# A decoder layer on one Trainium2 core: the second gate of the merge applied in the branch projection, sigmoids written as one plus tanh, and named buffers in place of a ring

## The chip, the cores and the metric

The kernel runs on one core of a Trainium2 chip. Its time is the device time of one launch in microseconds (us); for the kernel before, the median of three runs is 1783.04 us (1782.25 to 1786.08). The engines are named as the profile names them: PE multiplies matrices (PEld is its weight load), DVE and ACT work on vectors, POOL is the third vector engine and also issues some DMAs, and SP issues the other DMAs. A bank is one PSUM tile of 128x512 fp32, in which matmuls accumulate.

## The reference

One layer on 1024 positions of width 1024. What matters here is the gated merge of two attention branches:

```
proj = rms_norm(h) @ w_in                 # also gate_a, gate_b (1024 each)
o_a  = multi-head latent attention        # 1024 x 512
o_b  = stick-breaking attention           # 1024 x 512
merged = sigmoid(gate_a) * (o_a @ w_br_mla) + sigmoid(gate_b) * (o_b @ w_br_sb)
h = h + merged @ w_out
h = h + swiglu(rms_norm(h));  h = h + sigmoid(h @ w_ple_gate) * rms_norm(p @ w_ple_proj)
out = rms_norm(h)
```

## The kernel before

**Layout and precision.** Activations lie transposed: 128 features on the partitions, positions along the row, in two halves of 512. Every fp32 product is made of three matmuls on split operands: `split` (L130-132) writes a high part with a cast on ACT (L131) and the rest with a subtraction on DVE (L132), and `passes` (L134-139) multiplies high by high (L137), high by low (L138) and low by high (L139). One product over four blocks of 128 is thus 12 matmuls of 128x512.

**The order.** The code is written stage by stage; a scheduler sorts the instructions of each engine by a cost model and by priorities, and each engine then runs its list in order. A tile is a buffer from a pool; a tile whose tag has `bufs=n` shares n buffers in rotation, and a load into it waits until the earlier user is done. DMAs issued by SP and by POOL stand in the lists of these engines in the same way.

**The stages around the change.** In the input projection the two gates go to DRAM as `d_gate` (rows 0 to 1023 are gate_a, 1024 to 2047 gate_b); the stick-breaking attention leaves its heads in `d_oT`. Then comes the latent attention (MLA), head by head: `mla_proj` (L572) with weights loaded by SP (L537 w_q_b, L539 w_kv_b, one buffer for both), `mla_weights` (L601: scores, exponentials on ACT, a scaling on POOL at L637), `mla_values` (L642: transposes, casts, products). While it runs, `br_sb_unit` (L678-691) fills PE's gaps at a very low priority: for each of 8 blocks `dc` of 128 output features it loads a block of w_br_sb, splits it, and for each half makes 12 matmuls into a `pb` bank (the bank M, of which there is one), copies the bank to `bo` with ACT (L690), and stores `bo` to `d_br` by a DMA on POOL's queue (L691). The projected branch B, not yet gated, so waits in DRAM for the merge.

**The merge** works with the pool `bg`: eight slots of 16 KB per partition, one ring tag (L744-746), so that the n-th tile takes the slot that the (n-8)-th leaves. For each of four blocks `dc` of the first half of the features, `gates_in` (L753) loads a block of w_br_mla and fills one slot `gt` with gate_a, branch B and gate_b (L759, L760, L761; 512 KB each). `wo_units` (L764) loads blocks k of w_out into `woraw` (L769, two buffers) and splits them into slots `wo`. `merge` (L772) splits its weights, takes two sigmoids of 128x1024 on ACT (L778), multiplies the second with branch B on POOL (L779), and for each half makes a `pb` product of 12 matmuls, multiplies it by the first gate (DVE, L785), adds the gated branch (DVE, L786) and splits the sum into `mT`. When four blocks are merged, the products `po` of `mT` with `wo` (12 matmuls per bank, 16 banks) are made, added to the input (L808) and stored; this is the first half of the sum over k. The second half loads and merges blocks 4 to 7 while those run (L810-814), and its products come in `out_group` (L894, the addition at L903), among the start of the feed-forward stage. `pb` and `po` rotate through five banks.

The same ring later holds weights and activations (`wpj`, `spare`, `b1` to `b7`, `hs`, `wpg`).

Of the kernel before, what the change touches and what calls it, by code (L numbers as in the profile page):

```python
# [51 lines left out]
def decoder_layer(ctx: ExitStack, tc: tile.TileContext, x, p, positions, g_mix, w_in, g_q_a, w_q_b,  # L52
# [104 lines left out]
    with ExitStack() as att:  # L157
# [340 lines left out]

        with ExitStack() as ml:
            lastp = pool(late, "lastpair", side="right")  # L500
            oah = lastp.tile([P, S], F32R, name="oah")
            oal = lastp.tile([P, S], F32R, name="oal")

            def slot(tag, name, dtype=F32R):
                return qkp.tile([P, S], dtype, name=name, tag=tag, bufs=2 if tag == "vst" else 3)
# [172 lines left out]
            def br_sb_unit(dc):  # L678
                raw = bp.tile([P, 4, P], F32, name="braw", tag="braw", bufs=2)
                with tc.issue_after(fence[0]):  # L680
                    nc.sync.dma_start(out=raw, in_=w_br_sb[:, dc * P:(dc + 1) * P].rearrange("(k p) n -> p k n", p=P))
                wh = bp.tile([P, 4, P], F32R, name="bwh", tag="bwh", bufs=2)
                wl = bp.tile([P, 4, P], F32R, name="bwl", tag="bwl", bufs=2)
                split(wh, wl, raw)
                for hf in range(2):
                    s = slice(hf * HALF, (hf + 1) * HALF)
                    pb = ps.tile([P, HALF], F32, name="pb", **M)
                    passes(pb, [((wh[:, k, :], wl[:, k, :]), (obh[:, k, s], obl[:, k, s])) for k in range(4)])
                    go = bp.tile([P, HALF], F32, name="bo", tag="bo", bufs=2)
                    nc.scalar.copy(out=go, in_=pb)  # L690
                    nc.gpsimd.dma_start(out=d_br[dc * P:(dc + 1) * P, s], in_=go)  # L691

# [71 lines left out]
    def wo_units(kh):  # L764
        for k in range(4 * kh, 4 * kh + 4):
            if k % 2 == 0:
                wo[k // 2] = slot("wo", [P, 2, 2, D])
            raw = wk.tile([P, D], F32, name="woraw", tag="woraw", bufs=2)
            nc.sync.dma_start(out=raw, in_=w_out[k * P:(k + 1) * P, :])  # L769
            split(wo[k // 2][:, 0, k % 2, :], wo[k // 2][:, 1, k % 2, :], raw)  # L770

    def merge(dc, raw, g):  # L772
        kh = dc // 4
        wh = oap.tile([P, 4, P], F32R, name="wh", tag="wh", bufs=2)
        wl = oap.tile([P, 4, P], F32R, name="wl", tag="wl", bufs=2)
        split(wh, wl, raw)
        for i in range(2):
            nc.scalar.activation(out=g[:, i, :], in_=g[:, i, :], func=AF.Sigmoid)  # L778
        nc.gpsimd.tensor_tensor(out=g[:, 2, :], in0=g[:, 2, :], in1=g[:, 1, :], op=ALU.mult)  # L779
        for hf in range(2):  # L780
# [3 lines left out]
            u = g[:, 0, s]  # L784
            nc.vector.tensor_tensor(out=u, in0=pb, in1=u, op=ALU.mult)  # L785
            nc.vector.tensor_tensor(out=u, in0=u, in1=g[:, 2, s], op=ALU.add)  # L786
            split(mT[hf, kh][:, 0, dc % 4, :], mT[hf, kh][:, 1, dc % 4, :], u)
# [5 lines left out]

    gs = [gates_in(i) for i in range(4)]
    for hf in range(2):
        mT[hf, 0] = slot(f"mT{hf}0", [P, 2, 4, HALF])
    wo_units(0)
    for i in range(4):
        merge(i, *gs[i])

    gs1 = [gates_in(4 + i) for i in range(4)]
    for hf in range(2):
        for f in range(NK):
# [3 lines left out]
            out_products(po, 0, hf, f)  # L807
            nc.vector.tensor_tensor(out=st, in0=po, in1=st, op=ALU.add)  # L808
            nc.sync.dma_start(out=d_h[f * P:(f + 1) * P, hcol(hf)], in_=st)
    for hf in range(2):  # L810
        mT[hf, 1] = slot(f"mT{hf}1", [P, 2, 4, HALF])
    wo_units(1)
# [340 lines left out]
    for i in (1, 2, 6, 5, 7, 3, 4):  # L1153
# [125 lines left out]
```

## Time and profile before

| | |
|---|---|
| median of three runs | 1783.04 us (1782.25 to 1786.08) |
| the profiled execution | 1785.67 us, its span 1784.0 us |
| mean granted clock of PE | 0.981 |
| DMA traffic | 222.16 MB, mean 125 GB/s |
| MLA stage, with the filler `br_sb_unit` | about 560 to 819 us |
| first half of the merge, up to its last `pb` product | about 821 to 836 us |

The page of the profile gives busy times per engine over the whole span. A row of a timeline is: start, duration, engine, line, operation, output and inputs, count, and in brackets how long the engine had stood idle before it and what ended that. A row of a tile gives min/median/max of the durations in ns. A row of the windows gives the window, its length, then for each engine busy time and count of instructions, then the granted clock of PE (1.00 is full), the share of the DMA engines that was busy and GB/s. Matmuls overlap: the duration of one is longer than the distance from its start to the next.

### The profile page before, as it was taken

What the parts mean: (1) busy time and instruction counts of PE and PEld (TensorE: products, weight loads), DVE (VectorE), ACT (ScalarE), POOL (GpSimd) and SP (SyncE); (2) the same over time, 40 slices, a digit from 0 to 9 for tenths busy, and PEclk for the clock granted to TensorE, in tenths of its full rate; (3) what the DMA queues carried; (4) which work ended last, traced back from release to release, by engine and by line L of the source; (5) the groups of instructions that cost most, each with busy time, mean ns of one, the idle gap of its engine ahead of it and who ended that gap; (6) DMA issues with size and microseconds to landing.
All of it is one profiled execution on the core that took longest, in us unless ns stands there. A gap on an engine that the chain in (4) does not pass through costs nothing.

```text
span 1784.0 us, 23325 instructions
## 1 busy us (share of the span) xinstructions
PE 1697.2 (95%) x8148; PEld 1410.5 (79%) x8148; DVE 1157.2 (65%) x2063; ACT 901.7 (51%) x1748; POOL 389.7 (22%) x401
## 2 busy tenths in 40 slices
PE   6999999999998999996999899899999999999996
PEld 5888878888786888885889777688888878887795
DVE  6667788778885766686468765754444545557656
ACT  5266676767774777775335633233333334445411
POOL 2011320000210533342202623334434310000000
PEclk9999999999999999998999899999999999999998
DMA  5212221213314210215953475853223328565522
GB/s 171 55 58 48 59 60 42 82 45 90 115 42 138 72 61 31 83 58 200 346 205 115 143 257 180 277 168 100 95 89 118 113 101 300 191 198 164 165 67 79
DMA packets 168249, 222.16 MB, mean 125 GB/s; under 512 B 23170, under 2 KB 99970, under 8 KB 168130
## 3 DMA queue, kind: packets, MB, share of 16 engines
q1 hardware_dynamic: 162098, 200.73, 34.6%
q0 software_dynamic: 6032, 19.93, 3.1%
q8 instruction: 64, 1.05, 0.2%
q14 instruction: 55, 0.45, 0.1%
HBM read 151.93 MB, written 67.90 MB: 123 GB/s over the span
## 4 chain that ended last, share of the span: by engine, by line
PE 74%; DVE 9%; issue 6%; DMA 5%; POOL 2%; ACT 2%; SPq 1%; POOLq 0%; DVEq 0%; ACTq 0%
PE pt L137 5%; PE pt L138 5%; PE pt L139 5%; PE pd L138 4%; PE pd L137 4%; PE pd L139 4%; PE pP L139 3%; PE pP L137 3%; PE pP L138 3%; DMA spare<-w_ffn_down 2%; PE po L137 2%; PE tp L651 2%; PE po L138 2%; PE po L139 2%; PE pg L139 2%
## 5 line engine op out<-in xcount | busy, mean ns | idle before, releaser
L137 PE MATMUL pt<-nTh,w_h 128*128 128x512 f32 (+1 forms) x480 | 192.5, 402 | 3.4 <-ACT go L355 2.4
L138 PE MATMUL pt<-nTl,w_h 128*128 128x512 f32 (+1 forms) x480 | 190.1, 396 | 0.0
L139 PE MATMUL pt<-nTh,w_l 128*128 128x512 f32 (+1 forms) x480 | 189.0, 395 | 0.0
L132 DVE TENSOR_TENSOR wl<-raw,wl 128x512 fp32r<-128x512 f32 x132 | 95.4, 723 | 101.9 <-ACT wl L131 101.4
L139 PE MATMUL pP<-b,wl 128*128 128x512 f32 x352 | 139.8, 399 | 10.1 <-DVE wl L132 10.1
L131 ACT CAST wl<-raw 128x512 fp32r<-128x512 f32 x132 | 82.0, 622 | 129.2 <-PE pP L139 59.0
L137 PE MATMUL pP<-b,wl 128*128 128x512 f32 x352 | 140.2, 398 | 5.0 <-DVE t L968 3.2
L138 PE MATMUL pP<-b,wl 128*128 128x512 f32 x352 | 139.3, 396 | 0.0
L137 PEld LDWEIGHTS pt<-nTh,w_h 128*128 128x128 f32 (+1 forms) x480 | 90.7, 189 | 26.1 <-ACT go L355 5.8
L139 PEld LDWEIGHTS pt<-nTh,w_l 128*128 128x128 f32 (+1 forms) x480 | 90.6, 189 | 19.7
L138 PEld LDWEIGHTS pt<-nTl,w_h 128*128 128x128 f32 (+1 forms) x480 | 90.9, 189 | 18.5
L138 PE MATMUL pd<-drs,dls 128*128 128x512 f32 x296 | 102.0, 390 | 1.0 <-DVE drs L132 1.0
L139 PE MATMUL pd<-drs,dls 128*128 128x512 f32 x296 | 101.7, 389 | 0.0
L132 DVE TENSOR_TENSOR drs<-drr,drs 128x512 fp32r<-128x512 f32 x74 | 50.8, 690 | 78.1 <-ACT drs L131 78.1
L137 PE MATMUL pd<-drs,dls 128*128 128x512 f32 x296 | 100.7, 392 | 0.4 <-ACT dls L131 0.4
L131 ACT CAST drs<-drr 128x512 fp32r<-128x512 f32 x74 | 45.9, 623 | 105.0 <-PE pd L139 98.3
L637 POOL TENSOR_SCALAR pw<-pw,st 128x128 f32<-128x128 f32 (+5 forms) x48 | 75.0, 1569 | 71.6 <-DVE st L633 20.2
L139 PEld LDWEIGHTS pP<-b,wl 128*128 128x128 f32 x352 | 67.4, 192 | 28.2 <-DVE wl L132 13.9
L137 PEld LDWEIGHTS pP<-b,wl 128*128 128x128 f32 x352 | 67.7, 192 | 20.1 <-DVE t L968 4.1
L138 PEld LDWEIGHTS pP<-b,wl 128*128 128x128 f32 x352 | 67.6, 192 | 14.3
L445 DVE TENSOR_TENSOR sz<-sz,T 128x512 f32<-128x512 f32 (+2 forms) x96 | 52.2, 550 | 34.6 <-PE T L443 33.8
L356 POOL DMA_DIRECT2D d_gate<-go x32 | 17.8, 556 | 260.3 <-ACT go L355 221.2
(371 smaller groups left out, 4821.9 us busy)
## 6 DMA issues: line engine op xcount, KB each, us to landing
d_g<-t SPq DMA_DIRECT2D x74, 256.0 KB, 2.0
drr<-d_g SPq DMA_DIRECT2D x74, 256.0 KB, 2.8
w_raw<-w_in SPq DMA_DIRECT2D x33, 512.0 KB, 4.2
raw<-w_ffn_gate SPq DMA_DIRECT2D x11, 1024.0 KB, 5.6
raw<-w_ffn_up SPq DMA_DIRECT2D x11, 1024.0 KB, 5.5
spare<-w_ffn_down SPq DMA_DIRECT2D x44, 256.0 KB, 3.7
d_w<-spare SPq DMA_DIRECT2D x44, 256.0 KB, 3.6
drr<-d_w SPq DMA_DIRECT2D x44, 256.0 KB, 2.6
```

The lines of the kernel that those rows point to most:

```text
L131: nc.scalar.copy(out=h, in_=src)
L132: eng.tensor_tensor(out=l, in0=src, in1=r32(h), op=ALU.subtract)
L137: nc.tensor.matmul(ps, lhsT=ah, rhs=bh, start=first and i == 0, stop=False, **kw)
L138: nc.tensor.matmul(ps, lhsT=ah, rhs=bl, start=False, stop=False, **kw)
L139: nc.tensor.matmul(ps, lhsT=al, rhs=bh, start=False, stop=last and i == n - 1, **kw)
L356: nc.gpsimd.dma_start(out=dst, in_=go[0:rows, :])
L445: nc.vector.tensor_tensor(out=sz[:, c0:], in0=sz[:, c0:], in1=T[:, c0:], op=ALU.subtract)
L637: nc.gpsimd.tensor_scalar(out=pw[:, 0:nk], in0=pw[:, 0:nk], scalar1=st[:, 6:7], scalar2=None, op0=ALU.mult)
L651: nc.tensor.transpose(tp[:, i * P:(i + 1) * P], rows[i][:, kb * P:(kb + 1) * P], ident)
```

## The change

Line numbers of the changed kernel stand in square brackets.

1. **The second gate moves into `br_sb_unit`.** The unit loads its half of gate_b (256 KB, into `bo`, now three buffers, SP's queue, [L691]), ACT takes tanh(0.5 x) of it in place ([L692]), and DVE evacuates the bank with (tanh + 1) * pb in one instruction ([L697]), where ACT copied it before. POOL stores the result as before ([L698]). `d_br` now holds twice the gated branch.
2. **Sigmoids as one plus tanh.** sigmoid(x) is (1 + tanh(x/2)) / 2. In `merge` one tanh of 128x1024 on ACT ([L790]) replaces two sigmoids, the POOL product is gone, and DVE's (tanh + 1) * pb ([L796]) replaces the multiplication. The merged rows are twice too large; the factor 0.5 is put into the two additions behind the products `po` ([L819] and [L914], a scalar_tensor_tensor where a tensor_tensor was).
3. **Loads of the merge.** A `gt` slot now holds gate_a and gated branch B of two blocks, so four blocks take two slots, and gate_b isn't loaded there.
4. **The activation table** that holds exp and tanh is loaded at the start of the MLA stage ([L500]). The program has six table loads before and after; the one that stood ahead of the sigmoids (L778) is the one that is now at [L500].
5. **Named slots.** Each tile of `bg` names one of eight tags with one buffer each, so that it waits for one given predecessor: `gt` 0 and 1, `mT` of the first half 2 and 3, `wo` 4 and 5 (in both halves), `mT` of the second half 6 and 7; later `wpj` 3, `spare` 2, `b1, b2, b5, b6, b7, b3, b4` in 0, 1, 6, 7, 4, 5, 3, `hs` in 2, 3, 6, 7, `wpg` in 0, 1, 4, 5.

```diff
+            tc.keep_in_program_order(nc.scalar.preload_act_table_set("exp_and_others"))
...
                 split(wh, wl, raw)
+
+                go = []
+                for hf in range(2):
+                    go.append(bp.tile([P, HALF], F32, name="bo", tag="bo", bufs=3))
+                    with tc.issue_after(fence[0]):
+                        nc.sync.dma_start(out=go[hf], in_=d_gate[D + dc * P:D + (dc + 1) * P, hcol(hf)])
+                    nc.scalar.activation(out=go[hf], in_=go[hf], func=AF.Tanh, scale=0.5)
                 for hf in range(2):
                     s = slice(hf * HALF, (hf + 1) * HALF)
                     pb = ps.tile([P, HALF], F32, name="pb", **M)
                     passes(pb, [((wh[:, k, :], wl[:, k, :]), (obh[:, k, s], obl[:, k, s])) for k in range(4)])
-                    go = bp.tile([P, HALF], F32, name="bo", tag="bo", bufs=2)
-                    nc.scalar.copy(out=go, in_=pb)
-                    nc.gpsimd.dma_start(out=d_br[dc * P:(dc + 1) * P, s], in_=go)
+                    nc.vector.scalar_tensor_tensor(out=go[hf], in0=go[hf], scalar=1.0, in1=pb, op0=ALU.add, op1=ALU.mult)
+                    nc.gpsimd.dma_start(out=d_br[dc * P:(dc + 1) * P, s], in_=go[hf])
...
-    def slot(name, shape, dtype=F32R):
+    def slot(i, name, shape, dtype=F32R):
 
-        return bg.tile(shape, dtype, name=name, tag="big", bufs=8)
+        return bg.tile(shape, dtype, name=name, tag=f"big{i}", bufs=1)
...
-        t = slot("gt", [P, 4, S], F32)
-        ds = slice(dc * P, (dc + 1) * P)
-        nc.sync.dma_start(out=t[:, 0, :], in_=d_gate[ds, :])
-        nc.sync.dma_start(out=t[:, 2, :], in_=d_br[ds, :])
-        nc.sync.dma_start(out=t[:, 1, :], in_=d_gate[D + dc * P:D + (dc + 1) * P, :])
-        return raw, t
+        t = slot(i, "gt", [P, 2, 2, S], F32)
+        raws = []
+        for j in range(2):
+            ds = slice((dc + j) * P, (dc + j + 1) * P)
+            raws.append(w_in_branch(dc + j))
+            nc.sync.dma_start(out=t[:, j, 0, :], in_=d_gate[ds, :])
+            nc.sync.dma_start(out=t[:, j, 1, :], in_=d_br[ds, :])
+        return [(raws[j], t[:, j]) for j in range(2)]
...
-        for i in range(2):
-            nc.scalar.activation(out=g[:, i, :], in_=g[:, i, :], func=AF.Sigmoid)
-        nc.gpsimd.tensor_tensor(out=g[:, 2, :], in0=g[:, 2, :], in1=g[:, 1, :], op=ALU.mult)
+        nc.scalar.activation(out=g[:, 0, :], in_=g[:, 0, :], func=AF.Tanh, scale=0.5)
...
-            nc.vector.tensor_tensor(out=u, in0=pb, in1=u, op=ALU.mult)
-            nc.vector.tensor_tensor(out=u, in0=u, in1=g[:, 2, s], op=ALU.add)
+            nc.vector.scalar_tensor_tensor(out=u, in0=u, scalar=1.0, in1=pb, op0=ALU.add, op1=ALU.mult)
+            nc.vector.tensor_tensor(out=u, in0=u, in1=g[:, 1, s], op=ALU.add)
...
-            nc.vector.tensor_tensor(out=st, in0=po, in1=st, op=ALU.add)
+            nc.vector.scalar_tensor_tensor(out=st, in0=po, scalar=0.5, in1=st, op0=ALU.mult, op1=ALU.add)
...
-                nc.vector.tensor_tensor(out=h, in0=po[:, w], in1=h, op=ALU.add)
+                nc.vector.scalar_tensor_tensor(out=h, in0=po[:, w], scalar=0.5, in1=h, op0=ALU.mult, op1=ALU.add)
```

**How the instructions move.** First DVE's list at the end of the first half of the merge, before; L786 adds the gated branch, the rows with `wo` and `mT` are the low parts of splits (two `mT` tiles, one for each half of the positions), `wl` those of the next blocks' weights.

```order
L786 TENSOR_TENSOR gt<-gt 128x512 x2
L132 TENSOR_TENSOR wo<-woraw,wo 128x1024
L786 TENSOR_TENSOR gt<-gt 128x512 x2
L132 TENSOR_TENSOR wo<-woraw,wo 128x1024
L132 TENSOR_TENSOR wl<-raww,wh 128x512 x2
L132 TENSOR_TENSOR wo<-woraw,wo 128x1024
L132 TENSOR_TENSOR mT_8357<-gt,mT_8357 128x512
L132 TENSOR_TENSOR mT_8358<-gt,mT_8358 128x512
```

The same place after, from the last block's multiplications on.

```order
L796 SCALAR_TENSOR_TENSOR gt<-gt,pb 128x512 x2
L132 TENSOR_TENSOR mT_8384<-gt,mT_8384 128x512
L797 TENSOR_TENSOR gt<-gt 128x512
L132 TENSOR_TENSOR mT_8385<-gt,mT_8385 128x512
L797 TENSOR_TENSOR gt<-gt 128x512
L132 TENSOR_TENSOR wo<-woraw,wo 128x1024 x2
L132 TENSOR_TENSOR mT_8384<-gt,mT_8384 128x512
L132 TENSOR_TENSOR wl<-raww,wh 128x512 x2
L132 TENSOR_TENSOR mT_8385<-gt,mT_8385 128x512
L132 TENSOR_TENSOR wo<-woraw,wo 128x1024 x2
L819 SCALAR_TENSOR_TENSOR st<-po,st 128x512 x15
```

Before, every `mT` split stood behind all the additions and behind three `wo` splits; now the `mT` splits of the first three blocks stand between the additions, and the first two `wo` splits behind them.

Next PE's list where the first products `po` begin, before; the number behind `po` tells the banks apart, `mT00` is the merged block row of the first half, and L137, L138, L139 are the three passes.

```order
L137 MATMUL po_8567<-mT00_8357,wo_8359 128x512
L137 MATMUL po_8584<-mT00_8357,wo_8359 128x512
L137 MATMUL po_8601<-mT00_8357,wo_8359 128x512
L137 MATMUL po_8618<-mT00_8357,wo_8359 128x512
L137 MATMUL po_8635<-mT00_8357,wo_8359 128x512
L138 MATMUL po_8567<-mT00_8357,wo_8359 128x512
L139 MATMUL po_8567<-mT00_8357,wo_8359 128x512
L137 MATMUL po_8567<-mT00_8357,wo_8359 128x512
```

And after.

```order
L137 MATMUL po_8580<-mT00_8384,wo_8386 128x512
L138 MATMUL po_8580<-mT00_8384,wo_8386 128x512
L137 MATMUL po_8597<-mT00_8384,wo_8386 128x512
L138 MATMUL po_8597<-mT00_8384,wo_8386 128x512
L137 MATMUL po_8614<-mT00_8384,wo_8386 128x512
L138 MATMUL po_8614<-mT00_8384,wo_8386 128x512
L137 MATMUL po_8631<-mT00_8384,wo_8386 128x512
L138 MATMUL po_8631<-mT00_8384,wo_8386 128x512
L137 MATMUL po_8648<-mT00_8384,wo_8386 128x512
L138 MATMUL po_8648<-mT00_8384,wo_8386 128x512
L139 MATMUL po_8580<-mT00_8384,wo_8386 128x512
L137 MATMUL po_8580<-mT00_8384,wo_8386 128x512
```

The five banks now run ten matmuls on the high part of `wo` before the first that needs its low part (L139); it was six.

Last SP's list in the MLA stage, before: `braw` is the filler's weight block, `raw<-d_oT` the stick-breaking heads, w_q_b and w_kv_b the next head's weights.

```order
L681 DMA braw<-w_br_sb 128x4x128
L675 DMA raw<-d_oT 128x1024
L537 DMA raw<-w_q_b 128x3x96
L539 DMA raw<-w_kv_b 128x2x128
L681 DMA braw<-w_br_sb 128x4x128 x2
L537 DMA raw<-w_q_b 128x3x96
```

And after.

```order
L676 DMA raw<-d_oT 128x1024
L691 DMA bo<-d_gate 128x512
L682 DMA braw<-w_br_sb 128x4x128
L691 DMA bo<-d_gate 128x512
L538 DMA raw<-w_q_b 128x3x96
L540 DMA raw<-w_kv_b 128x2x128
L691 DMA bo<-d_gate 128x512
L682 DMA braw<-w_br_sb 128x4x128
L691 DMA bo<-d_gate 128x512
L538 DMA raw<-w_q_b 128x3x96
```

Each loaded half of gate_b stands between the filler's weights and the next head's weights. Since `bo` has three buffers, such a load waits in SP's list until an earlier half has been stored, and the loads behind it wait too.

More of the change, by code (lines that the diff above doesn't have):

```diff
@@ L751, in decoder_layer, with w_in_branch, gates_in @@
     wk = pool(mg, "merge")
-    def gates_in(dc):
+    def w_in_branch(dc):
         raw = oap.tile([P, 4, P], F32, name="raww", tag="raww", bufs=2)
         nc.sync.dma_start(out=raw, in_=w_br_mla[:, dc * P:(dc + 1) * P].rearrange("(k p) n -> p k n", p=P))
-        t = slot("gt", [P, 4, S], F32)
-        ds = slice(dc * P, (dc + 1) * P)
-        nc.sync.dma_start(out=t[:, 0, :], in_=d_gate[ds, :])
-        nc.sync.dma_start(out=t[:, 2, :], in_=d_br[ds, :])
-        nc.sync.dma_start(out=t[:, 1, :], in_=d_gate[D + dc * P:D + (dc + 1) * P, :])
-        return raw, t
+        return raw
+    def gates_in(i, dc):
+        t = slot(i, "gt", [P, 2, 2, S], F32)
[6 more added lines that the diff above has]
+        return [(raws[j], t[:, j]) for j in range(2)]
     def wo_units(kh):
@@ L766, in wo_units @@
             if k % 2 == 0:
-                wo[k // 2] = slot("wo", [P, 2, 2, D])
+                wo[k // 2] = slot(4 + k // 2 % 2, "wo", [P, 2, 2, D])
             raw = wk.tile([P, D], F32, name="woraw", tag="woraw", bufs=2)
@@ L792, in out_products @@
                      (mT[hf, kh][:, 0, k % 4, c], mT[hf, kh][:, 1, k % 4, c])) for k in range(4 * kh, 4 * kh + 4)])
-    gs = [gates_in(i) for i in range(4)]
+    gs = [g for i in range(2) for g in gates_in(i, 2 * i)]
     for hf in range(2):
-        mT[hf, 0] = slot(f"mT{hf}0", [P, 2, 4, HALF])
+        mT[hf, 0] = slot(2 + hf, f"mT{hf}0", [P, 2, 4, HALF])
     wo_units(0)
@@ L799, in decoder_layer @@
         merge(i, *gs[i])
-    gs1 = [gates_in(4 + i) for i in range(4)]
+    gs1 = [g for i in range(2) for g in gates_in(i, 4 + 2 * i)]
     for hf in range(2):
@@ L807, in decoder_layer @@
             out_products(po, 0, hf, f)
[L808 removed]
+            nc.vector.scalar_tensor_tensor(out=st, in0=po, scalar=0.5, in1=st, op0=ALU.mult, op1=ALU.add)
             nc.sync.dma_start(out=d_h[f * P:(f + 1) * P, hcol(hf)], in_=st)
     for hf in range(2):
[L811 removed]
+        mT[hf, 1] = slot(6 + hf, f"mT{hf}1", [P, 2, 4, HALF])
     wo_units(1)
@@ L850, in decoder_layer @@
             nc.sync.dma_start(out=hs[f, hf], in_=d_h[f * P:(f + 1) * P, hcol(hf)])
-    wpj = slot("wpj", [P, 2, 2, D])
+    wpj = slot(3, "wpj", [P, 2, 2, D])
     pw = []
@@ L890, in decoder_layer @@
     embed_in()
-    spare = slot("spare", [P, 8, HALF], F32)
+    spare = slot(2, "spare", [P, 8, HALF], F32)
     t2 = [spare[:, 4 + kk, :] for kk in range(4)]
@@ L938, in decoder_layer @@
     for i in (1, 2, 5, 6, 7, 3, 4):
-        Bn[i] = slot(f"b{i}", [P, 2, 4, HALF])
+        Bn[i] = slot({1: 0, 2: 1, 5: 6, 6: 7, 7: 4, 3: 5, 4: 3}[i], f"b{i}", [P, 2, 4, HALF])
     for f in range(NK):
@@ L1189, in decoder_layer @@
         if i == 6:
-            hsp = {(1, a): slot("hs", [P, 2, 4, HALF]) for a in range(2)}
-            wpg = [slot("wpg", [P, 2, 2, NK, P]) for _ in range(4)]
-            hsp.update({(0, a): slot("hs", [P, 2, 4, HALF]) for a in range(2)})
+            hsp = {(1, a): slot(2 + a, "hs", [P, 2, 4, HALF]) for a in range(2)}
+            wpg = [slot((0, 1, 4, 5)[a], "wpg", [P, 2, 2, NK, P]) for a in range(4)]
+            hsp.update({(0, a): slot(6 + a, "hs", [P, 2, 4, HALF]) for a in range(2)})
     def hidden(f, hf):
```

## The prediction

> **What bounds the kernel now.** I read the page's busy times first, then PE's waits, then stretches around the longest wait the change touches.
>
> ```profile
> PE 1697.2 (95%) x8148; PEld 1410.5 (79%) x8148; DVE 1157.2 (65%) x2063; ACT 901.7 (51%) x1748; POOL 389.7 (22%) x401
> ...
> PE po L137 <- ACT mT L131: 11.4, 1, 11.4
> PE pR L139 <- DVE wl L132: 5.8, 1, 5.8
> ```
>
> PE is busy 95% of the span, and the change removes no matmul. It can gain only where PE waits or runs at a lower clock, and it loses wherever a new step holds PE up. The largest single wait of PE is the change's own place: the first product `po` waits 11.4 us for the split merged rows.
>
> ```profile
> 820.81 1.22 PE L137 MATMUL pb<-oah,wh 128*128 128x512 f32 x2 [2.04 <-ACT oah L131]
> 835.81 0.39 PE L139 MATMUL pb<-oah,wl 128*128 128x512 f32 x1
> 847.56 2.50 PE L137 MATMUL po<-mT,wo 128*128 128x512 f32 x5 [11.37 <-ACT mT L131]
> 850.72 0.46 PE L137 MATMUL po<-mT,wo 128*128 128x512 f32 x1
> 851.48 0.39 PE L137 MATMUL po<-mT,wo 128*128 128x512 f32 x1
> 854.88 0.39 PE L137 MATMUL po<-mT,wo 128*128 128x512 f32 x1
> ```
>
> From 851.48 to 854.88 fifteen matmuls follow each other: 0.2267 us each at full clock. The last `pb` matmul starts at 835.81, so that work ends at 836.04. The first 60 `po` matmuls (five banks of 12) are 13.6 us and would end at 849.64 without a wait. Seven of them start before 850.72; the other 53 end at 850.72 + 53 x 0.2267 = 862.7. The place loses 13.1 us, of which about 1.6 is low clock.
>
> Who holds the rows back is read from the three other engines.
>
> ```profile
> 823.98 1.28 ACT L778 ACT_TABLE_LOAD   x1
> 825.28 6.75 ACT L778 ACTIVATE gt<-gt 128x1024 f32<-128x1024 f32 x7
> 827.37 10.39 POOL L779 TENSOR_TENSOR gt<-gt 128x1024 f32<-128x1024 f32 x4 [24.16 <-ACT gt L778]
> 840.03 1.28 DVE L786 TENSOR_TENSOR gt<-gt 128x512 f32<-128x512 f32 x2
> 841.23 1.21 DVE L132 TENSOR_TENSOR wo<-woraw,wo 128x1024 fp32r<-128x1024 f32 x1
> 842.37 1.28 DVE L786 TENSOR_TENSOR gt<-gt 128x512 f32<-128x512 f32 x2
> 842.47 2.67 SPq L769 DMA_DIRECT2D woraw<-w_out  x2
> 845.95 1.04 ACT L131 CAST wo<-woraw 128x1024 fp32r<-128x1024 f32 x1 [8.02 <-DMA woraw<-w_out]
> 846.90 4.25 ACT L131 CAST mT<-gt 128x512 fp32r<-128x512 f32 x8
> ```
>
> ACT loads a table and takes sigmoids one after another, POOL multiplies until 837.8, and DVE's additions end only past 843. The low part of `wo` block 0 stands on DVE among these additions (841.23), so its raw buffer comes free late and block 2 is loaded at 842.47; ACT's cast of block 2 stands ahead of the first `mT` cast and waits for that load. The row named as the releaser is thus the end of a line that starts with the sigmoids.
>
> **A, the opening of the merge.** ACT's second `wh` cast ends just before the table load, at about 823.97. After it now comes one tanh (a sigmoid of the same size, row L778 below: 1.06), so DVE starts at about 825.2. Its list up to the third block's last addition is 16 operations of 128x512. Starts are (841.23 - 840.03) / 2 = 0.60 apart, so they end at 834.8; the multiply-add form is taken at that price, since the last two of the following rows have the two forms alike.
>
> ```profile
> L778 ACT ACTIVATE gt<-gt x16: 1042/1060/1064, 825.3 to 869.8; 128x1024 f32<-128x1024 f32 x16
> ...
> L785 DVE TENSOR_TENSOR gt<-pb,gt 128x512 f32<-128x512 f32 x16 | 10.6, 686 | 5.7 <-PE pb L139 3.3 <-ACT gt L778 2.3
> L227 DVE SCALAR_TENSOR_TENSOR q<-pt,q 64x512 fp32r<-64x512 f32 x16 | 11.0, 687 | 6.3 <-ACT q L226 5.9
> ```
>
> Then ACT casts the last of these rows and `wo` block 0, whose high part is ready at 836.7. PE restarts at about 836.9 instead of 847.56: gap 0.9. Ten matmuls need only high parts of block 0 and end at 839.2. DVE meanwhile does six more operations, two of them not before the last `pb` at 836.04, then the low part (842.37 - 841.23 = 1.14): ready at 840.6, gap 1.5. Twenty matmuls last until 845.2. Raw block 2 can be loaded only when block 0 leaves its buffer at about 840.5.
>
> ```profile
> DMA to landing us min/median/max: 3.5/5.7/11.1
> ```
>
> That is the row of `woraw`. With fewer loads in flight than before I take 4.6, between its least and its median, and 1.05 for the cast: 846.4, gap 1.2. The three gaps make 3.6, so A gains 13.1 - 3.6 = **9.5**. Ends: no gap at all, 13.1; a raw block that lands after 11.1, 6.5 later, 3.0.
>
> The removed loads (four of 512 KB in each half) and the POOL product are inside this sum; the second half's run under the products `po` and `out_group`, where PE has work, and count nothing. The two 0.5 factors replace instructions of the same shape and count nothing.
>
> **B, the opening of the MLA stage.** The moved table load lies in front of ACT's first work there.
>
> ```profile
> 561.65 0.59 ACT L355 COPY go<-pt 128x512 f32<-128x512 f32 x1 [5.23 <-PE pt L139]
> L690 ACT COPY bo<-pb x16: 577/586/616, 592.3 to 741.2; 128x512 f32<-128x512 f32 x16
> L691 POOL DMA_DIRECT2D d_br<-bo x16: 542/595/618, 593.5 to 742.1; - x16
> DMA to landing us min/median/max: 2.3/2.4/4.7
> ```
>
> ACT idles 5.23 us there, which hides the 1.28; if that idle time is not where the load lands, it costs 1.3. The three loads of gate_b that go ahead in SP's list (256 KB each; the nearest rows, a store of that size, land in 2.4 us) and up to three tanhs fall into the stage's start, where weights are awaited. I take +1, from 0 to +3.
>
> **C, the body of the MLA stage.** ACT's 16 copies (last row but one: 0.586) become 16 tanhs of the same shape: nothing by count. DVE gets 16 new evacuations of about 0.69 (L785, L227): 11.0 us, spread over 592 to 741.
>
> ```profile
> 600.00:620.00 20.00, 20.00 (x114) 17.22 (x113) 13.46 (x34) 13.82 (x34) 7.41 (x10) 1.00 0.25 81
> 661.84 0.37 SPq L537 DMA_DIRECT2D raw<-w_q_b  x1
> 655.54 0.59 POOL L691 DMA_DIRECT2D d_br<-bo  x1
> PE pk L137 <- ACT wh L131: 2.7, 1, 2.7
> ```
>
> PE is full here, DVE 13.46 of 20, so 11 us in 150 fit beside it unless they delay `tl` or the single bank M; if that cover is gone, they cost at most 11. The new wait is the tanh's: it stands in ACT's list, and ACT's casts for the attention stand behind it. It waits for a load that waits in SP's list for one of three buffers, that is for the product, the evacuation, POOL's issue (0.59) and a landing of 2.4. Behind the load in SP's list stand the next head's w_q_b weights. The store at 655.54 lands at about 658.5 (655.54 + 0.59 + 2.4), and the next weights were issued at 661.84, so this queue has some 3 us to spare. By the same working I find a tanh short of its load in about four places by up to 2 us, mostly absorbed by ACT's idle third. I take +2, from 0 to +8.
>
> **D, slots and later order.** The named slots change the order of DVE, POOL and SP at the start of the feed-forward stage, where one row (L132 `wl`, 5.8 us) is the largest wait in reach. Nothing says which way: 0, from -3 to +3.
>
> **Sum.** -9.5 + 1 + 2 + 0 = **-6.5**. The profiled execution took 1785.67 us (its span 1784.0 and 1.67 around it), 2.6 above the median; from it, 1779.2. From the median of 1783.04 it is 1776.5, my forecast.
>
> **A rule weighed: the clock.**
>
> ```profile
> 479.76 0.79 PE L137 MATMUL pt<-nTh,w_h 128*128 128x512 f32 x1 [1.67 <-ACT go L355]
> 485.78 0.40 PE L139 MATMUL pt<-nTh,w_l 128*128 128x512 f32 x1
> 1051.72 0.50 PE L137 MATMUL pP<-b,wl 128*128 128x512 f32 x1 [1.75 <-DVE spare L968]
> 820.00:825.00 5.00, 4.19 (x10) 3.24 (x11) 2.18 (x4) 2.87 (x4) 0.00 (x0) 0.51 0.94 367
> ```
>
> After a gap of 1.67 at 479.76 the long matmul form stays until 485.78, 6 us at about half speed, worth 3.0 us; the window at 820 shows a clock of 0.51 after a gap of 2.04. After 1.75 at 1051.72 the form is short at once. My gaps of 0.9, 1.5 and 1.2 lie below all three. The Trainium skill (TensorE: Matmul & The Clock Gate, section "HAM oscillation — how this bites in real kernels") sets the limit for idle gaps at about 3.4 us. By it my sum would stay at -6.5 with no clock loss; by the first and the last of these rows, not by the third, one loss of 3.0 is possible. The trace of before speaks against the rule as a safe limit, so the loss is a rival.
>
> **The rivals.** About 0.2% (3.6 us) is what a measurement of this kernel can tell from no change.
>
> 1. *The clock drops once after a new gap.* -6.5 + 3.0 = -3.5: 1779.5, at the edge between faster and same. For it: 479.76; against: 1051.72, and gaps that are shorter. Chance 0.08.
> 2. *The wait moves on to the raw `wo` blocks.* There are still two raw buffers, so blocks 2 and 3 land late: A gains 3.0, and B and C give back 3: 1783.0. For it: 845.95, where exactly such a load ended an 8.02 us wait of ACT. Against: the loads of `gt` that shared the DMAs are fewer. Chance 0.12.
> 3. *Slower: tanhs stall ACT in the MLA stage.* Each tanh that comes at the last moment waits for issue, landing and its own load: 0.59 + 2.4 + 2.4 = 5.4 us (estimate from the rows of `bo`). ACT is idle 31% of the window at 600, so of the 9.3 us between two tanhs (149 / 16) some 2.9 absorb it; 2.5 remain, times 13 halves without a fresh buffer: 33 us at most. It turns the result slower once PE loses over (9.5 - 1 + 3.6) / 13 = 0.93 us at each. At half the ceiling: 1783.04 - 9.5 + 1 + 16 = 1790.5. For it: `PE pk` already waited 2.7 us for such weights, and SP's list is strictly in order. Against: three buffers, and a queue with 3 us to spare. Chance 0.10.
> 4. *The change doesn't do what it says.* Were the table reloaded between exp and tanh, 16 more pairs at 1.28 would cost 41 us of ACT. The instruction lists have as many loads after as before, so this is left at under 0.02.
>
> **How the numbers follow.** The forecast case has 0.68, the rivals 0.08, 0.12 and 0.10, all else 0.02. Range: downward the whole 13.1 and 3 of D, 1783.04 - 16.1 = 1767; upward past rival 2 by about 2 of C or D, 1785; outside lie most of rival 3 and little else. Faster: 0.68 and half of the edge case, **0.72**; same: 0.12, the other half and a little of the rest, **0.17**; slower: 0.10 and a little, **0.11**. The likeliest time is **1776.5**, the range **1767** to **1785**.
>
> **What would show it.** A: PE's wait for `po` shrinks from 11.4 to at most 2, the products restart at 837, and three gaps summing to 3 to 4 us follow within 10 us. B: PE's busy time from 560 to 592 is unchanged within 1 to 3 us. C: PE stays at 20 of 20 in windows of the MLA stage, and ACT's idle time before L692, ended by the load of `bo`, is below 2 us each time. I am wrong if the last `pb` ends later than now relative to the stage's start (C or B larger), if `po` waits over 3 us for `wo` (rival 2), if half-clock matmuls last over 3 us after 837 (rival 1), or if w_q_b's issues in SP's list slip by several us against the scores of their head (rival 3).

## The result and the profile after

The changed kernel took 1766.19 us (median of four runs, 1764.39 to 1770.78) against 1783.88 us for the kernel before; the ratio is 0.9908, with a 95% interval of 0.9888 to 0.9928. It is faster by 17.7 us, where 6.5 were forecast, and 0.8 us below the low end of the range; two of the four runs (1767.61 and 1770.78) lie inside it.

PE's busy time on the page, and its waits, after:

```profile
PE 1689.8 (96%) x8148; PEld 1406.3 (80%) x8148; DVE 1159.9 (66%) x2079; ACT 893.1 (51%) x1740; POOL 368.1 (21%) x393
...
PE pP L137 <- ACT wl L131: 3.5, 1, 3.5
...
PE po L137 <- ACT wo L131: 2.2, 2, 1.5
...
PE pk L137 <- DVE bo L697: 0.8, 2, 0.6
...
PE pR L137 <- DVE spare L979: 0.6, 1, 0.6
PE po L139 <- DVE wo L132: 0.6, 1, 0.6
```

The wait of 11.4 us for the merged rows is 2.2 + 0.6 now, and the 5.8 us of `pR` at the start of the feed-forward stage have become 0.6. A new wait stands there too: the first product `pP` of that stage waits 3.5 us for the cast of its weights. The opening of the merge on PE, DVE and ACT:

```profile
818.12 1.22 PE L137 MATMUL pb<-oah,wh 128*128 128x512 f32 x2 [2.04 <-ACT oah L131]
831.78 0.39 PE L139 MATMUL pb<-oah,wl 128*128 128x512 f32 x1
833.63 0.50 PE L137 MATMUL po<-mT,wo 128*128 128x512 f32 x1 [1.45 <-ACT wo L131]
836.77 0.50 PE L139 MATMUL po<-mT,wo 128*128 128x512 f32 x1 [0.58 <-DVE wo L132]
842.37 0.50 PE L137 MATMUL po<-mT,wo 128*128 128x512 f32 x1 [0.74 <-ACT wo L131]
```

```profile
822.28 1.28 DVE L796 SCALAR_TENSOR_TENSOR gt<-gt,pb 128x512 f32<-128x512 f32 x2 [0.27 <-ACT gt L790]
831.89 1.28 DVE L796 SCALAR_TENSOR_TENSOR gt<-gt,pb 128x512 f32<-128x512 f32 x2
```

```profile
832.53 2.00 ACT L131 CAST wo<-woraw 128x1024 fp32r<-128x1024 f32 x2
```

DVE's first 16 operations run from 822.28 to 831.89, without a pause; then ACT casts `wo` block 0 and PE goes on. The three gaps sum to 2.8 us.

For the whole program I cut both profiles at the same counted matmuls, so that each stretch holds the same work. The rows are: the MLA stage (first `pk` to 241st `pb`), the merge (to the 61st `po`), the second half (to the last `po`), the products `pp` behind it, the start of the feed-forward stage (to the 61st `pR`), and its end (last `pQ` to first `pg`). First the kernel before, then the changed one.

```profile
564.31:823.53 259.22, 251.95 (x1376) 211.47 (x1377) 184.58 (x434) 185.34 (x433) 89.90 (x81) 0.99 0.20 68
823.53:862.81 39.28, 27.91 (x109) 22.46 (x108) 29.50 (x36) 23.43 (x29) 13.21 (x6) 0.83 0.92 333
862.81:961.34 98.53, 98.53 (x531) 85.41 (x529) 59.52 (x101) 32.55 (x52) 8.70 (x5) 1.00 0.61 217
961.34:997.14 35.80, 35.53 (x210) 30.54 (x209) 27.42 (x69) 20.53 (x43) 18.79 (x6) 1.00 0.43 151
997.14:1120.18 123.04, 110.65 (x470) 89.52 (x469) 77.98 (x112) 48.84 (x89) 46.49 (x30) 0.94 0.60 200
1447.95:1671.16 223.21, 219.05 (x955) 178.14 (x953) 129.10 (x210) 95.96 (x170) 3.39 (x2) 1.00 0.61 200
```

```profile
560.31:820.85 260.54, 253.93 (x1377) 212.98 (x1377) 194.78 (x450) 185.35 (x433) 88.77 (x81) 0.98 0.27 89
820.85:849.30 28.45, 25.67 (x109) 20.24 (x108) 22.36 (x34) 17.12 (x22) 0.00 (x0) 0.99 0.91 324
849.30:947.84 98.54, 98.54 (x531) 85.43 (x529) 59.19 (x103) 28.74 (x47) 1.74 (x2) 1.00 0.58 199
947.84:982.62 34.78, 34.34 (x202) 29.94 (x201) 28.50 (x71) 25.98 (x58) 13.43 (x6) 1.00 0.41 144
982.62:1100.26 117.64, 109.63 (x479) 89.14 (x477) 77.99 (x111) 43.78 (x77) 54.44 (x29) 0.96 0.64 211
1428.78:1650.02 221.24, 218.55 (x954) 178.32 (x953) 128.54 (x209) 95.32 (x169) 3.39 (x2) 1.00 0.62 202
```

By stage: the MLA stage +1.3, the merge -10.8, the second half 0.0, the products behind it and the start of the feed-forward stage -1.0 and -5.4, the end of that stage -2.0. The profiled executions differ by 21.3 us (1785.67 and 1764.39), more than the medians: 4.0 of it lie before the MLA stage (its first `pk` at 564.31 and 560.31), in code that is the same in both. PE's busy time from 95.5 us up to there is 460.6 and 456.8 us, at granted clocks of 0.99 and 1.00: some microseconds at half clock come and go between executions, and I don't count them to the change. The part of the feed-forward stage between the last two rows is 0.8 us longer.

### The profile page after: what moved, and what is told of

The parts are those of the page before. It is cut to its first block, busy times and chain, and to the rows that moved or that the text cites. A ratio compares the mean times of both kernels' runs of the same rounds, so it can differ in the third digit from the quotient of the medians.

```text
span 1762.7 us, 23332 instructions
## 1 busy us (share of the span) xinstructions
PE 1689.8 (96%) x8148; PEld 1406.3 (80%) x8148; DVE 1159.9 (66%) x2079; ACT 893.1 (51%) x1740; POOL 368.1 (21%) x393
## 4 chain that ended last, share of the span: by engine, by line
PE 72%; DVE 9%; issue 7%; DMA 7%; ACT 2%; POOL 2%; SPq 0%; POOLq 0%; DVEq 0%; ACTq 0%
PE pt L137 5%; PE pt L138 5%; PE pt L139 5%; PE pd L138 3%; PE pd L137 3%; PE pd L139 3%; PE pP L139 3%; PE pP L137 3%; PE pP L138 3%; DMA spare<-w_ffn_down 2%; PE pQ L137 2%; PE pQ L138 2%; PE pg L137 2%; PE pQ L139 2%; PE pg L139 2%
## 5 line engine op out<-in xcount | busy, mean ns | idle before, releaser
L137 PE MATMUL pt<-nTh,w_h 128*128 128x512 f32 (+1 forms) x480 | 190.8, 398 | 3.5 <-ACT go L355 2.4
L138 PE MATMUL pt<-nTl,w_h 128*128 128x512 f32 (+1 forms) x480 | 188.5, 393 | 0.0
L139 PE MATMUL pt<-nTh,w_l 128*128 128x512 f32 (+1 forms) x480 | 187.6, 392 | 0.0
L132 DVE TENSOR_TENSOR wl<-raw,wl 128x512 fp32r<-128x512 f32 x132 | 98.7, 750 | 97.5 <-ACT wl L131 97.0
L139 PE MATMUL pP<-b,wl 128*128 128x512 f32 x352 | 139.0, 397 | 11.4 <-DVE wl L132 11.4
L137 PE MATMUL pP<-b,wl 128*128 128x512 f32 x352 | 139.6, 397 | 5.7 <-ACT wl L131 3.5
L138 PE MATMUL pP<-b,wl 128*128 128x512 f32 x352 | 139.4, 396 | 0.0
L137 PEld LDWEIGHTS pt<-nTh,w_h 128*128 128x128 f32 (+1 forms) x480 | 89.7, 187 | 25.7 <-ACT go L355 5.9
L139 PEld LDWEIGHTS pt<-nTh,w_l 128*128 128x128 f32 (+1 forms) x480 | 89.8, 187 | 19.2
L138 PEld LDWEIGHTS pt<-nTl,w_h 128*128 128x128 f32 (+1 forms) x480 | 89.9, 187 | 18.2
L138 PE MATMUL pd<-drs,dls 128*128 128x512 f32 x296 | 100.7, 390 | 0.1
L139 PE MATMUL pd<-drs,dls 128*128 128x512 f32 x296 | 100.4, 389 | 0.0
L137 PE MATMUL pd<-drs,dls 128*128 128x512 f32 x296 | 99.9, 392 | 0.0
L139 PEld LDWEIGHTS pP<-b,wl 128*128 128x128 f32 x352 | 67.2, 191 | 29.8 <-DVE wl L132 15.9
L137 PEld LDWEIGHTS pP<-b,wl 128*128 128x128 f32 x352 | 67.4, 192 | 20.4 <-ACT wl L131 3.8
L138 PEld LDWEIGHTS pP<-b,wl 128*128 128x128 f32 x352 | 67.4, 191 | 14.2
L356 POOL DMA_DIRECT2D d_gate<-go x32 | 17.7, 554 | 260.2 <-ACT go L355 218.3
```

Source lines behind the costliest of these rows:

```text
L132: eng.tensor_tensor(out=l, in0=src, in1=r32(h), op=ALU.subtract)
L137: nc.tensor.matmul(ps, lhsT=ah, rhs=bh, start=first and i == 0, stop=False, **kw)
L138: nc.tensor.matmul(ps, lhsT=ah, rhs=bl, start=False, stop=False, **kw)
L139: nc.tensor.matmul(ps, lhsT=al, rhs=bh, start=False, stop=last and i == n - 1, **kw)
L356: nc.gpsimd.dma_start(out=dst, in_=go[0:rows, :])
```

## The experiments

The first question was which part gave what. Theory N: the gates gave the merge's gain, and the named slots, independently, the gain later on. Rival R: all of it follows from the gates. The table holds, for each kernel, the ratio to the kernel before (with its interval) and the lengths of the stages in its profile, cut as above; "start" is the products `pp` and the start of the feed-forward stage together. About 4.6 us of ring's 168.2 there are lost in 10 us at about half clock (shown in the last section).

| kernel | ratio | MLA | merge | second half | start | end |
|---|---|---|---|---|---|---|
| before | 1 | 259.2 | 39.3 | 98.5 | 158.8 | 223.2 |
| changed | 0.9908 (0.9888 to 0.9928) | 260.5 | 28.4 | 98.5 | 152.4 | 221.2 |
| ring | 1.0021 (1.0003 to 1.0039) | 263.3 | 37.1 | 98.5 | 168.2 | 223.3 |
| before_named | 0.9997 (0.9983 to 1.0011) | 258.1 | 40.4 | 98.5 | 160.7 | 221.4 |
| late_gate | 0.9948 (0.9931 to 0.9965) | 257.9 | 38.0 | 98.7 | 152.9 | 221.4 |
| bo2 | 0.9917 (0.9895 to 0.9939) | 263.1 | 28.3 | 98.5 | 154.6 | 221.2 |
| late_pair | 0.9907 (0.9894 to 0.9921) | 262.3 | 28.1 | 98.6 | 153.2 | 221.3 |
| late_pair2 | 0.9928 (0.9911 to 0.9946) | 262.8 | 30.1 | 98.6 | 154.8 | 221.4 |
| act_back | 0.9905 (0.9886 to 0.9924) | 262.3 | 29.2 | 98.6 | 155.0 | 221.7 |
| act_pool_back | 0.9965 (0.9952 to 0.9977) | 262.5 | 35.1 | 98.7 | 154.6 | 221.3 |
| woraw4 | 0.9948 (0.9933 to 0.9963) | 262.5 | 28.4 | 98.5 | 162.3 | 221.3 |
| woraw3 | 0.9943 (0.9926 to 0.9960) | 262.6 | 27.4 | 98.7 | 160.8 | 221.1 |
| after_wl | 0.9917 (0.9900 to 0.9934) | 262.0 | 28.4 | 98.6 | 152.6 | 221.3 |
| ring_list | 0.9942 (0.9920 to 0.9964) | 262.2 | 28.5 | 99.4 | 159.1 | 223.0 |
| before_list | 1.0009 (0.9996 to 1.0023) | 258.7 | 33.5 | 106.1 | 161.4 | 223.3 |

**ring: the gates without the names.** In the changed kernel:

```diff
-        return bg.tile(shape, dtype, name=name, tag=f"big{i}", bufs=1)
+        return bg.tile(shape, dtype, name=name, tag="big", bufs=8)
```

> The changed kernel with one ring of eight slots again in place of the named slots; gates and tanh stay changed. Theory N (two independent gains: the gates give the merge's 10.8 us back and cost 1.3 in the MLA stage, the names give some 6 us at the start of the feed-forward stage and 2 to 3 at its end): about 1783.9 - 10.8 + 1.3 = 1774, some us more if blocks of w_out wait for ring slots in the second half, and PE waits over 4 us again at the start of the feed-forward stage. Rival R (the later gain is a consequence of the gates): about 1766, no such wait.

Measured: no faster than before, 1.0021. The merge gained only 2.2 us, so theory N fell in its first part, and the rival with it: the gates alone, on the ring and with its lists, give nothing. PE waits 8.26 us for the merged rows, and ACT's rows tell for what:

```profile
847.90 2.50 PE L137 MATMUL po<-mT,wo 128*128 128x512 f32 x5 [8.26 <-ACT mT L131]
```

```profile
846.28 1.04 ACT L131 CAST wo<-woraw 128x1024 fp32r<-128x1024 f32 x1 [6.22 <-DMA woraw<-w_out]
847.23 4.25 ACT L131 CAST mT<-gt 128x512 fp32r<-128x512 f32 x8
```

All eight casts of the merged rows stand in ACT's list behind a cast of a `wo` block that waits for its load, although the first rows had long been added up. It is the picture of the kernel before (its rows at 845.95 and 846.90), with the sigmoids and POOL's product gone.

**before_named: the names without the gates.** The same diff the other way, with `gt` in slots `dc % 4`, and each later tile in the slot that the ring gave it.

> The kernel before with eight named slots, each tile owning the slot that the ring gave it; nothing else changed. Theory N: about 1783.9 - 6 - 2.5 = 1775, the wait of PE for the merged rows stays at 11.4 us, the 5.8 us wait at the start of the feed-forward stage goes. Rival R: 1784, all waits as before.

Measured: 0.9997, no change. The end of the feed-forward stage gained the 2 us, its start nothing, and the merge nothing, although the loads of `gt` for the first four blocks were issued before the MLA stage ended (the last at 804.14). No cast that waits for a load stands ahead of the merged rows in ACT's list here, and still PE waits 11.18 us:

```profile
844.35 0.80 PE L137 MATMUL po<-mT,wo 128*128 128x512 f32 x1 [11.18 <-ACT wo L131]
```

The cast of `wo` block 0 (843.26) stands behind the casts of the third block's merged rows, which DVE adds up until 842.7, a pair of additions taking 3.3 us beside POOL's product. In the changed kernel ACT's list has the same order there, and that cast comes at 832.53.

Both one-part kernels stay at the old time, and the two parts together give 17 us: neither gain was independent.

**late_gate: tanh and names, but the second gate still in the merge.** On top of before_named, with the table's load, the first gate's form and the factors 0.5 of the changed kernel; the second gate reads:

```diff
-            nc.scalar.activation(out=g[:, i, :], in_=g[:, i, :], func=AF.Sigmoid)
-        nc.gpsimd.tensor_tensor(out=g[:, 2, :], in0=g[:, 2, :], in1=g[:, 1, :], op=ALU.mult)
+            nc.scalar.activation(out=g[:, i, :], in_=g[:, i, :], func=AF.Tanh, scale=0.5)
+        nc.vector.scalar_tensor_tensor(out=g[:, 2, :], in0=g[:, 1, :], scalar=1.0, in1=g[:, 2, :], op0=ALU.add, op1=ALU.mult)
```

> Named slots as in before_named, table preloaded and one plus tanh in the merge, but the second gate still applied there: ungated branch stored, gate_b loaded in the merge, and (tanh + 1) * branch on DVE in place of POOL's product. Theory P (table load, POOL and sigmoids made the line; DVE now has four more operations of 1.1 to 1.2 us and ACT four more tanhs): the merge gains 4 to 7 of the 10.8 us, about 1769 to 1771. Rival L (the loads of gate_b and the slots they fill held the line): nothing gained in the merge, 1775 as before_named.

Measured: the merge is 38.0, a gain of 1.3 from before where theory P gave 4 to 7, so rival L's "nothing" came nearer. PE restarts sooner, after 4.61 us, but waits twice more:

```profile
838.33 0.79 PE L137 MATMUL po<-mT,wo 128*128 128x512 f32 x1 [4.61 <-ACT wo L131]
849.67 0.50 PE L137 MATMUL po<-mT,wo 128*128 128x512 f32 x1 [2.86 <-ACT wo L131]
859.10 0.50 PE L137 MATMUL po<-mT,wo 128*128 128x512 f32 x1 [2.32 <-DVE st L809]
```

```profile
842.20 4.85 ACT L779 ACTIVATE gt<-gt 128x1024 f32<-128x1024 f32 x5
847.27 1.06 ACT L779 ACTIVATE gt<-gt 128x1024 f32<-128x1024 f32 x1 [0.22 <-DMA gt<-d_gate]
848.57 1.05 ACT L131 CAST wo<-woraw 128x1024 fp32r<-128x1024 f32 x1 [0.24 <-DMA woraw<-w_out]
```

With twice the tanhs, six of the second half's stand in ACT's list ahead of `wo` block 2. Taking the second gate out of the merge is worth about 10 us of its length here (38.0 against 28.4; the slots' numbers differ too), beyond the table load and POOL's product. The kernel is faster than before all the same, 0.9948, by the start (-5.9) and the end (-1.8) of the feed-forward stage.

**bo2: two buffers for the halves of gate_b.**

```diff
-                    go.append(bp.tile([P, HALF], F32, name="bo", tag="bo", bufs=3))
+                    go.append(bp.tile([P, HALF], F32, name="bo", tag="bo", bufs=2))
```

> The changed kernel with two buffers for the halves of gate_b in the MLA stage in place of three, so that each load waits for an older store. If the tanh's load has slack in the stage (the stage cost only 1.3 us): within 2 us of the changed kernel, 1765 to 1768. Rival 3 of the prediction (tanhs at the last moment stall ACT): the MLA stage is longer by over 5 us, 1771 or more.

Measured: 0.9917, and an MLA stage of 263.1, which lies among those of the other kernels with the new gates (260.5 to 263.3). ACT now waits seven times for such a load, at most 2.1 us, and the stage isn't longer for it. The loads have slack; the rival that tanhs stall ACT is out.

**late_pair and late_pair2: late loads.** Theory T, formed on ring: the ring lets only the first `gt` slot be loaded during the MLA stage, and loads after its end keep PE waiting. In late_pair the second slot's loads were placed behind an instruction of the MLA stage in the lists:

```diff
+        if dc == 2:
+            with tc.issue_after(fence[1]):
+                return gate_loads(i, dc)
```

> The changed kernel, but the loads of the second gt slot (blocks 2 and 3 of the first half) wait for the last copy of the MLA stage, as they do with the ring; all else as changed. Theory T (two lines held the merged rows, the late loads of the ring and the computation of the second gate; either alone keeps most of the wait): the merge, 28.4 us from its first new product to the 60th product po, grows to 34 to 37 us, about 7 us slower than the changed kernel, 1773 to 1776. Rival V (the ring's cost lay elsewhere, the late loads are covered): 28 to 30 us, within 2 us of the changed kernel.

This didn't delay them (SP issued them from 801.83 on), so the run only repeats the changed kernel: 0.9907. late_pair2 makes them wait for data, by writing one column of each with rows that the MLA stage makes last:

```diff
+        if dc == 2:
+            for j in range(2):
+                for m in range(2):
+                    nc.gpsimd.tensor_copy(out=t[:, j, m, 0:1], in_=oah[:, S - 1:S])
```

> The changed kernel, but four one-column writes on POOL, which read the last rows of the MLA stage, stand ahead of the four loads of the second gt slot, so that these start some 1 to 2 us later than the ring lets them start. Theory T (late loads alone keep most of the wait): the merge takes 34 to 38 us against 28.4, and the kernel is 6 to 10 us slower than the changed one. Rival V (late loads are covered): 28 to 31 us.

Measured: the loads went out from 824.41 on, some 23 us later than in late_pair, and the merge took 30.1, only 1.7 more than 28.4. Theory T fell: the loads are nearly covered.

**act_back and act_pool_back: the removed work put back.** The values stay.

```diff
+        nc.scalar.copy(out=g[:, 1, :], in_=g[:, 1, :])
+        nc.gpsimd.tensor_scalar(out=g[:, 1, :], in0=g[:, 1, :], scalar1=1.0, scalar2=None, op0=ALU.mult)
```

The first line alone is act_back.

> The changed kernel with one more ACT copy of 128x1024 in each merge step, in place on the gated branch (the value stays), as long as the sigmoid that went. Four of them (about 1 us each) lie in the opening of the merge. If ACT's second sigmoid was a main part of the line: the merge grows by 3 to 4 us. If DVE's row of operations sets the pace: by less than 1.5 us.

> As act_back, and POOL multiplies the gated branch by one behind the copy, as POOL's product did (four of 2.4 to 3 us in the opening). If POOL's row sets the line that the change removed: the merge grows by 7 us or more over the changed kernel, to 35 us or more, although the loads come early. If the loads alone did it: by less than 3 us. The instruction lists at the start of the feed-forward stage are here those of before_named: if these lists decide, PE idles there 12 to 14 us (8 with the changed kernel's lists, which act_back has).

Measured: act_back 29.2, so ACT's second function costs 0.7 of the merge; act_pool_back 35.1, so POOL's row, with the lists that the scheduler makes around it, costs 5.9 more. Here is that row, and DVE beside it:

```profile
829.29 5.52 POOL L792 TENSOR_SCALAR gt<-gt 128x1024 f32<-128x1024 f32 x2 [22.74 <-ACT gt L791]
835.37 6.02 POOL L792 TENSOR_SCALAR gt<-gt 128x1024 f32<-128x1024 f32 x2 [0.56 <-ACT gt L791]
```

```profile
832.10 2.12 DVE L799 TENSOR_TENSOR gt<-gt 128x512 f32<-128x512 f32 x2 [0.62 <-POOL gt L792]
837.38 1.28 DVE L799 TENSOR_TENSOR gt<-gt 128x512 f32<-128x512 f32 x2
846.88 1.28 DVE L799 TENSOR_TENSOR gt<-gt 128x512 f32<-128x512 f32 x2
```

The first pair of DVE's additions waits for POOL and takes 2.12 us beside it; a later one, at 837.38, takes 1.28 beside it. The last pair comes at 846.88, 5.5 us after POOL's end at 841.4. DVE isn't idle in between: the pair stands in its list behind the third block's additions, the split of a `wo` block, the next block's weight splits and two `mT` splits. So POOL's work and the order made for it aren't told apart here.

The other part of what was expected, on the start of the feed-forward stage, missed: PE idles 11.8 us there, not 12 to 14, and act_back 11.0, not 8, with the changed kernel's lists. From 30 us before that stage to its end the instructions of all engines stand in the same order in act_pool_back as in before_named, and yet the stage takes 154.6 and 160.7 us (before_named first):

```profile
959.59:1120.29 160.70, 146.93 (x680) 120.94 (x678) 109.20 (x181) 70.18 (x134) 64.78 (x35) 0.95 0.55 186
960.69:1115.31 154.62, 142.84 (x679) 117.86 (x678) 107.31 (x181) 69.64 (x134) 65.86 (x35) 0.98 0.57 194
```

Of the 6.1 us, 4.1 are PE's busy time, longer at the lower clock, and 2.0 its idle time. The order of the lists alone doesn't set the length of this stage.

**woraw4 and woraw3: more raw buffers for w_out.** Two became four, and three.

> The changed kernel with four raw buffers for w_out in place of two. The gaps of 0.58 and 0.74 us at blocks 0 and 2 remain of the wait for po; the one of 0.74 should go: 0.5 to 1 us faster, about 1765. Rival: the lists change elsewhere, and the start of the feed-forward stage moves by some us either way.

> The changed kernel with three raw buffers for w_out. The merge stays within 1 us of 28.4. The list of DVE at the start of the feed-forward stage has the additions for w_ffn_down ahead of the weight splits in longer rows, as with four buffers: if the lists decide, that stage is 4 to 9 us longer than the changed kernel's, as it was with four; if the four buffers themselves did it, within 2 us.

Measured: the merge stays (28.4 and 27.4), though the gap of 0.74 is gone in woraw4, but the start of the feed-forward stage is 9.9 and 8.4 us longer than the changed kernel's. Nothing in that stage uses these buffers; what the change moves there is the order of the lists. So the rival stated for woraw4 came true. Of the 9.9 us, 6.1 are idle time of PE and 3.8 are busy time at a lower clock; of the 8.4 they are 5.2 and 3.2. How much of it the order alone explains is open, as act_pool_back shows.

**after_wl: only the lists of that stage.** A higher priority for the weight splits of its first units.

> The changed kernel with a higher priority for the weight splits of the first feed-forward units: only the lists at the start of that stage change, two of DVE's five next weight splits move ahead of additions for w_ffn_down and the others behind. If these lists alone decide some us there: the first 36 blocks of the stage move by 3 us or more, the merge stays at 28.4. If they don't: within 1.5 us of the changed kernel in that stage.

Measured: 152.6 against 152.4. These two lists cost the same; not every shuffle matters.

**ring_list and before_list: ACT's list alone.** What was open after late_pair2 was why the ring kept 8 us in the merge. The split of blocks 2 and 3 of w_out is put behind the casts of the merged rows, in ring and in the kernel before:

```diff
+            if k in (2, 3):
+                with tc.issue_after(last_cast[-1]):
+                    split(wo[k // 2][:, 0, k % 2, :], wo[k // 2][:, 1, k % 2, :], raw)
```

> The ring of eight slots with the changed gates, as in ring, but the splits of blocks 2 and 3 of w_out are put behind the casts of the merged rows in ACT's list (the first two splits stay free). Theory Q (in ring the wait comes from ACT's list, where all casts of mT stand behind the cast of block 2, which waits for a raw buffer): the merge falls from 37.1 to 29 to 32 us, about what late_pair2 with its late loads has. Rival S (the ring's slots themselves come free late): 35 to 37 us.

> The kernel before with the same move in ACT's list and nothing else: ring, sigmoids, table load, POOL's products as before. If the list alone held the merged rows: the merge falls from 39.3 to 30 to 32 us, 7 to 9 us faster. If POOL's row holds them as well (its last product ended at 837.8, and act_pool_back says so): 34 to 37 us, 2 to 5 us faster.

Measured: ring_list has a merge of 28.5, all of the changed kernel's gain, on the ring. Theory Q holds: the names matter there only because the scheduler, with the ring, puts the casts behind the `wo` cast. before_list has 33.5, between its two forecasts: the list alone is worth 5.7 us of the merge, the gates the other 5. But before_list isn't faster at all (1.0009), since the second half gives it back:

```profile
856.84:962.91 106.07, 101.33 (x530) 87.20 (x530) 61.05 (x104) 34.98 (x54) 11.46 (x6) 0.97 0.65 231
```

```profile
PE po L138 <- DVE st L816: 4.7, 1, 4.7
```

PE now waits for a `po` bank that DVE frees late: 106.1 against 98.5. What makes DVE late there wasn't taken further apart.

## Why the prediction was wrong

- **What bounds the kernel** was read rightly: PE is full, and the gain is in its waits. The wait for `po` was the largest, and it went.
- **A, the opening of the merge** (-9.5): right, -10.8. DVE's 16 operations took 831.89 - 822.28 = 9.61 us, 9.6 were worked out; the gaps were 1.45, 0.58 and 0.74 where 0.9, 1.5 and 1.2 were expected. The working held because the instruction lists were read from the changed kernel. Its reason was only half of it: the row at 845.95, a cast waiting for a load, was called the end of a line that starts with the sigmoids. ring shows that it keeps 8.3 us of wait without them, by its place in ACT's list, and before_named that the work keeps 11.2 where no cast waits for a load ahead of the merged rows. Each of two holds kept most of the wait, and the change took away both.
- **B and C, the MLA stage** (+3): the pair of profiles says +1.3; over all profiles it is the mean 262.4 of the eleven kernels whose gates are applied in the branch projection against 258.5 of the four others, +3.9. Ten of the eleven have a wait of PE for ACT (`tv`, 10 us into the stage) of 1.9 us, which the changed kernel's own profile lacks: that belongs to B. The tanh's waits were foreseen in size and number: ACT's wait for the load of `bo`, below, is four times, at most 1.5.

```profile
ACT bo L692 <- DMA bo<-d_gate: 3.7, 4, 1.5
```

- **The moved table load** cost nothing; it ran in ACT's idle time at 552.43.

```profile
552.43 1.28 ACT L500 ACT_TABLE_LOAD   x1
```

- **D, slots and later order, is the step that failed** ("Nothing says which way: 0, from -3 to +3"). It measured -8.4: -6.4 up to the 61st `pR` and -2.0 at the end. The other terms, -10.8 and +3.9, make -6.9, near the -6.5 of the forecast. The 2 us at the end come with the named slots: every kernel with names has 221.1 to 221.7 there, every one with the ring 223.0 to 223.3. Of the 6.4, by the rows of the two profiles above, 4.2 are idle time of PE (12.7 us before, 8.5 after) and 2.2 are busy time, longer before at the lower clock. The wait of 5.8 us goes with the names: all four kernels with the ring have one of 5.5 to 5.8 us there, no kernel with names has it (their longest wait of `pR` for such a split is 2.1), and each of these waits 2.6 to 4.7 us at the first `pP` instead. In the kernel before DVE made 13 splits of `b` in a row ahead of a weight split that PE waited for; in the changed kernel the splits of `b` and the weight splits behind them come earlier:

```profile
1007.40 4.97 DVE L132 TENSOR_TENSOR b<-spare,b 128x256 fp32r<-128x256 f32 x8
1012.29 3.09 DVE L132 TENSOR_TENSOR b<-t,b 128x512 fp32r<-128x512 f32 x5
...
1019.58 0.68 DVE L132 TENSOR_TENSOR wl<-raw,wl 128x512 fp32r<-128x512 f32 x1
```

```profile
991.74 1.89 DVE L132 TENSOR_TENSOR wl<-raw,wl 128x512 fp32r<-128x512 f32 x3
```

The names bring this order, but the gain isn't theirs alone: before_named has nearly the same rows and 160.7, act_pool_back the order of before_named and 154.6, and woraw4 loses 9.9 with names and gates. What else sets the length of this start stays open. The range was too narrow for it: it was drawn around one wait of 5.8 us, stopped at -3, and left out that PE idled 12.7 us in this stretch.
- **Rival 1, the clock:** not seen. The merge's window has a granted clock of 0.99, and after the gap of 1.45 the next matmuls are at full speed. The Trainium skill (TensorE: Matmul & The Clock Gate, section "HAM oscillation — how this bites in real kernels") sets the limit for idle gaps at about 3.4 us, and the gap of 1.45 agrees with it. A gap of 2.62 us in late_gate, at the start of the feed-forward stage, was followed by half clock (a matmul of 0.79 us), so a gap below 3.4 us is not safe in every case.

```profile
1000.62 0.79 PE L137 MATMUL pP<-b,wl 128*128 128x512 f32 x1 [2.62 <-ACT wl L131]
```

- **Rival 2, the raw `wo` blocks:** a gap of 0.74, nothing more. **Rival 3, tanhs that stall ACT:** out, by bo2 and the row above. **Rival 4** was out by the lists.

## What to carry to other kernels

Where a scheduler makes the lists, a wait has two owners: the work that is late and the place in the list of what waits. Take one away and the other may keep all of it; test each alone and both together before a gain is credited to a part. A change of buffers reorders lists far away, and where PE waits there for several microseconds already, such a term has a range of the whole wait, in both directions.

## What the runs showed of the hardware

The clock can drop with no gap at all: in ring PE was busy throughout and ran at half clock for 10 us, while one-column matmuls (`pm`, eight in a row) were interleaved with wide ones; in the changed kernel the same products ran at full clock (the row 947.84:982.62 above).

```profile
993.00:998.00 5.00, 5.00 (x19) 4.24 (x19) 5.00 (x11) 1.43 (x3) 5.00 (x1) 0.58 0.14 52
998.00:1003.00 5.00, 5.00 (x18) 4.23 (x17) 0.99 (x2) 1.08 (x2) 1.88 (x1) 0.50 0.28 105
```

Such a drop cost before_named 3.1 us among these products and act_pool_back nothing, with the same instructions in the same order; stages of two profiles are compared better with their clocks beside them. And DVE can be slower beside POOL: in the kernel before a pair of additions took 5.70 us while POOL multiplied two tiles, where 1.28 is usual. Beside POOL's product with a constant, in act_pool_back, one pair took 2.12 us and another 1.28.

```profile
829.82 5.70 DVE L786 TENSOR_TENSOR gt<-gt 128x512 f32<-128x512 f32 x2 [0.26 <-POOL gt L779]
```
